# A fused encoder layer: one conv tap per fused pair on ScalarE, 64 fused pairs for 61, turned probabilities in the bias tile

## The chip, the cores and the metric

The kernel runs on one core of one Trainium2 chip, one launch for the whole layer. The metric is the time of the launch on the device in microseconds (us): 1574.34 us before, the median of 3 runs (1571.43 to 1574.68). All data are fp32; TensorE multiplies in its fp32r form, and each number is split into a high half and a low half, so that a product is three matmuls: high by high, low by high, high by low.

## The reference, cut to what matters

One encoder layer on 256 rows of 4096 columns. After a norm comes one projection of 4096 to 14336 columns, whose parts feed a convolution branch and an attention branch; both are gated, put side by side, and projected back to 4096.

```python
xn = rms_norm(x, norm_g[l])
h = jnp.einsum('bsd,de->bse', xn, w_in[l])                       # 256x4096 by 4096x14336
c_val, c_glu, c_gate, q, k, v, a_gate = jnp.split(h, split_pts, axis=-1)   # 7 x 2048
conv_out = conformer_conv(c_val, c_glu, ...) * jax.nn.silu(c_gate)   # GLU, depthwise conv of 31 taps, LayerNorm, SiLU
q = rms_norm(q.reshape(B, S, 16, 128), q_norm_g[l]); k = rms_norm(...)
attn = longnet_mixture(q, k, v, rel_bias)                        # 16 heads, three dilated windows, T5 bias
mixed = jnp.concatenate([conv_out, attn * jax.nn.silu(a_gate)], axis=-1)
x = x + jnp.einsum('bse,ed->bsd', mixed, w_out[l])               # 256x4096 by 4096x4096
```

In the kernel the three windows of the attention are one softmax over a 256x256 matrix of scores per head, with the pattern's weight folded into the bias.

## The kernel before

**Groups and pairs.** The weights of both projections are cut into 18 groups of 1024 columns, g0 to g17: four of the convolution's values and gates (g0 to g3), two of its outer gate (g4, g5), eight that alternate between queries with keys (`qk`) and attention gates with values (`agv`) in the order qk0, qk1, agv0, qk2, agv1, qk3, agv2, agv3 (g6 to g13), and four of the output projection (g14 to g17). A group has 16 pairs; a pair is 2x128 rows of weights by 1024 columns, loaded as one `raw` tile of 1 MB (`load_pair`, three tiles in flight). Its slot is its place in the group, its unit `u` is 16 times the group plus the slot, and the tiles carry the unit in their names (`wh219`). The group's four results, 128x512 each, stay in four PSUM banks while its 16 pairs go by; the other four banks (`side`) serve small matmuls of the side work.

**Plain and fused pairs.** A plain pair is 24 matmuls of 128x512: ScalarE casts the high half `wh` (L1027, two of 1024 columns), VectorE subtracts to get the low half `wl` (L1033, 2048 columns). A fused pair (`split_fused`, `fused`) multiplies its 2x2 blocks in the Strassen-Winograd way, with 7 products and so 21 matmuls; VectorE and ScalarE have to make sums of blocks for it, in four steps: `b` (one), `b22` (two), `t13` (three) and `t42` (four), each a cast on ScalarE and a subtraction on VectorE, with additions on VectorE between them (L1059, L1071, L1072), and four more PSUM banks hold its sums, so a group has no side banks while its fused pairs run. The sums of the rows' blocks come from `block_sums` once (`xs`, `xsp`). Before, groups 2 to 7 have six fused pairs, at slots 2, 4, 6, 8, 10 and 12, group 14 has four, and groups 15 to 17 have seven each, at slots 2, 4, 6, 8, 10, 12 and 13: 61 in all. Group 1 is plain and multiplies rows that aren't yet normalised; during it `split_xn` scales each of the 32 tiles of rows by its norm (L288, VectorE), casts (`nh`, L293, ScalarE) and subtracts (`nl`, L295).

**Side work and its order.** Everything else (the convolution, the attention, the gates, the splitting of the output projection's rows) is written as generators that wait in lanes. A planner emits them between the pairs: `credit` adds to `left[0]` (VectorE) and `left[1]` (ScalarE) for each matmul emitted (`PRODUCT`, 227 ns each, by the shares in `FILL`), `spend` takes off what an emitted operation is reckoned to cost, and `SAVED` is the most that can be kept. `pump` steps through the lanes; a lane steps while both its engines' credit is above zero. The order in which the operations are emitted is the order on each engine, and each engine takes its own queue in that order; weights are split ahead of their use as soon as `stream.step` finds storage: four tiles of 2048 columns, so a plain pair's halves are ready at most about one pair ahead, and four more of 1024 columns in the stretch of a group with fused pairs.

**The convolution's taps.** The 31 taps times four blocks of channels less the middle ones are 120 taps. Each is done either on VectorE (`conv_gen`, four operations L538) or on ScalarE (`conv_products`, four activations L500 into one of two `cp` buffers, then one addition L529 on VectorE). The lane `cp_lane` is stepped by `pump` and, in a fused pair, by step two of `split_fused`, after the cast of `b22`; a tap takes two steps.

**A head.** `head_gen` loads a Toeplitz tile of bias `T` (tag "toep", four buffers, 384 columns) over SP's queue, multiplies queries by keys into a side bank (`psc`, L701), adds bias (`pr`, L711), takes exponentials and scales on ScalarE (L718, L728), turns 32x32 blocks on VectorE (L734, into a tile `turn_p` of tag "t2", six buffers of 512 columns), writes that to DRAM and reads it back into `pr` over GpSimd's queue (`through_dram`), and multiplies by the values (`po`, L745).

## Time and profile before

| what | value |
|---|---|
| median of 3 runs | 1574.34 us (1571.43 to 1574.68) |
| the profiled execution | 1575.07 us |
| its span in the trace | 1573.3 us |
| TensorE busy (PE) | 1563.0 us, 99% |
| VectorE busy (DVE) | 1332.2 us, 85% |
| ScalarE busy (ACT) | 906.4 us, 58% |
| GpSimd busy (POOL) | 99.1 us, 6% |
| mean traffic of the DMA queues | 227 GB/s |

The span is from the first to the last record of the core; the profiled execution's time, measured as in the other runs, is 1.8 us longer. PE is TensorE, PEld its loads of stationary data, DVE VectorE, ACT ScalarE, POOL GpSimd, SP the engine whose queue issues most DMAs. A busy matmul record is longer than the step between two matmuls, since they are pipelined; how often a matmul starts is read from the starts or from windows. An arrow (`<-`) in brackets names what ended the idle time of the engine ahead of a row.

### The profile page before, as it was taken

To read this page: it belongs to the slowest core of one execution; us is meant where nothing else is said; L and a number is where in the kernel's file an instruction comes from. 1 tells how busy PE (TensorE), PEld (TensorE's weight loads), DVE (VectorE), ACT (ScalarE), POOL (GpSimd) and SP (SyncE) were. 2 spreads that over 40 slices of the span, in tenths; PEclk is the share of its full clock that TensorE was granted. 3 is DMA by queue.
4 is the path that set the end of the run, shared out by engine and by line. 5 is a ranking of instruction groups with operands and counts; after the bars stand their busy time and mean duration, and the time that the engine had idled before them with its cause. 6 is when DMAs were issued, how large, how long until landed. Compare 5 with 4: busy or idle time off the path is not lost.

```text
span 1573.3 us, 18566 instructions
## 1 busy us (share of the span) xinstructions
PE 1563.0 (99%) x6883; PEld 1293.3 (82%) x6883; DVE 1332.2 (85%) x1574; ACT 906.4 (58%) x1354; POOL 99.1 (6%) x184
## 2 busy tenths in 40 slices
PE   9999999999999999999999999999999999999999
PEld 8888788888888888888888887888888888888887
DVE  6667899989899998999878878888866788999988
ACT  6755554555455545667665775575565644555453
POOL 0000000000000000001202013021120300000000
PEclk9999999999999999999999999999999999999999
DMA  9766556555555565657967479566785765666663
GB/s 379 293 224 253 201 214 221 210 211 194 216 216 205 206 236 205 228 204 231 289 212 248 178 237 264 184 213 233 242 258 193 252 224 197 241 241 240 221 245 123
DMA packets 64523, 357.22 MB, mean 227 GB/s; under 512 B 9104, under 2 KB 11920, under 8 KB 27824
## 3 DMA queue, kind: packets, MB, share of 16 engines
q1 hardware_dynamic: 54096, 326.38, 58.3%
q0 software_dynamic: 10048, 29.37, 6.2%
q8 instruction: 54, 0.88, 0.2%
q10 hardware_dynamic: 288, 0.28, 0.1%
q14 instruction: 37, 0.30, 0.1%
HBM read 337.09 MB, written 18.91 MB: 226 GB/s over the span
## 4 chain that ended last, share of the span: by engine, by line
PE 98%; DMA 1%; issue 1%; DVE 1%; ACT 0%; POOL 0%; DVEq 0%; POOLq 0%
PE c L1226 44%; PE c L1228 22%; PE m L1197 5%; PE c L1242 4%; PE m L1199 3%; PE c L1244 2%; PE acc L929 2%; PE acc L930 2%; PE acc L932 2%; PE c L1088 2%; PE c L1089 2%; PE c L1197 2%; PE c L1090 2%; PE po L745 1%; PE m L1088 1%; PE c L1199 1%
## 5 line engine op out<-in xcount | busy, mean ns | idle before, releaser
L1033 DVE TENSOR_TENSOR wl<-raw,wh 128x2048 fp32r<-128x2048 f32 x211 | 482.8, 2289 | 155.5 <-ACT wh L1027 152.9
L1027 ACT CAST wh<-raw 128x1024 fp32r<-128x1024 f32 x422 | 421.3, 1048 | 241.7 <-PE c L1228 161.6
L1226 PE MATMUL c<-wh,nh 128*128 128x512 f32 x1152 | 449.1, 390 | 0.0
L1228 PE MATMUL c<-wh,nl 128*128 128x512 f32 x1152 | 448.2, 389 | 0.0
L1226 PE MATMUL c<-wl,nh 128*128 128x512 f32 x1152 | 285.9, 390 | 1.8 <-DVE wl L1033 1.8
L1050 ACT CAST t<-raw 128x1024 fp32r<-128x1024 f32 x122 | 128.5, 1053 | 267.0 <-DVE raw L1059 199.5
L1226 PEld LDWEIGHTS c<-wl,nh 128*128 128x128 f32 x1152 | 216.2, 188 | 47.1 <-DVE wl L1033 2.2
L1226 PEld LDWEIGHTS c<-wh,nh 128*128 128x128 f32 x1152 | 216.2, 188 | 44.9
L1228 PEld LDWEIGHTS c<-wh,nl 128*128 128x128 f32 x1152 | 216.2, 188 | 44.8
L1051 DVE TENSOR_TENSOR t<-raw,t 128x1024 fp32r<-128x1024 f32 x122 | 149.0, 1221 | 3.3
L538 DVE SCALAR_TENSOR_TENSOR cT<-a,wT,cT 128x255 f32<-128x255 f32 (+14 forms) x364 | 150.1, 471 | 0.3
L1226 PE MATMUL c<-wh,mh 128*128 128x512 f32 x280 | 109.1, 390 | 0.0
L1228 PE MATMUL c<-wh,ml 128*128 128x512 f32 x280 | 108.9, 389 | 0.0
L1059 DVE TENSOR_TENSOR raw<-raw 128x1024 f32<-128x1024 f32 x61 | 74.7, 1225 | 2.1
L1051 DVE TENSOR_TENSOR b<-raw,b 128x1024 fp32r<-128x1024 f32 x61 | 74.3, 1218 | 0.1
L1226 PE MATMUL c<-wl,mh 128*128 128x512 f32 x280 | 69.1, 389 | 0.0
L1050 ACT CAST b<-raw 128x1024 fp32r<-128x1024 f32 x61 | 63.9, 1047 | 1.3 <-DMA raw<-in_w_dram 0.9
L1226 PEld LDWEIGHTS c<-wl,mh 128*128 128x128 f32 x280 | 52.6, 188 | 10.9
L1226 PEld LDWEIGHTS c<-wh,mh 128*128 128x128 f32 x280 | 52.6, 188 | 10.9
L1228 PEld LDWEIGHTS c<-wh,ml 128*128 128x128 f32 x280 | 52.6, 188 | 10.9
L1197 PE MATMUL m<-t,xsp 128*128 128x512 f32 x180 | 60.3, 389 | 0.0
L1003 DVE TENSOR_TENSOR wh<-raw,wh 128x1024 fp32r<-128x1024 f32 x31 | 37.9, 1224 | 26.1 <-ACT wh L1002 25.9
(329 smaller groups left out, 2210.2 us busy)
## 6 DMA issues: line engine op xcount, KB each, us to landing
raw<-in_w_dram SPq DMA_DIRECT2D x286, 1024.0 KB, 4.9
xT<-in_x_cols_dram SPq DMA_DIRECT2D x15, 512.0 KB, 6.9
x<-in_x_dram SPq DMA_DIRECT2D x8, 512.0 KB, 7.8
xr<-in_x_dram SPq DMA_DIRECT2D x8, 512.0 KB, 6.5
out_dram<-xr SPq DMA_DIRECT2D x15, 256.0 KB, 7.0
T<-bias_dram SPq DMA_DIRECT2D x16, 192.0 KB, 6.4
raw<-in_w_dram SPq DMA_DIRECT2D x3, 512.0 KB, 6.0
turn_qk0d<-turn_qk POOLq DMA_DIRECT2D x2, 512.0 KB, 5.9
```

What stands on the lines that cost most here:

```text
L538: nc.vector.scalar_tensor_tensor(c[:, t, lo:hi], a[:, t, lo + sh : hi + sh], wT[:, 4 * cb + t, k : k + 1], c[:, t, lo:hi], op0=ALU.mult, o ...
L1027: nc.scalar.copy(h, raw_tiles[u][:, k])
L1033: nc.vector.tensor_sub(l, src, h.bitcast(F32))
L1050: nc.scalar.copy(h, src)
L1051: nc.vector.tensor_sub(l, src, h.bitcast(F32))
L1059: nc.vector.tensor_add(r[:, 0:4:3, :], r[:, 0:3:2, :], twice(r[:, 3, :]))
L1088: nc.tensor.matmul(acc, a[0], b[0], start=start, stop=False)
L1197: nc.tensor.matmul(acc, ah, b, start=begin, stop=end)
L1199: nc.tensor.matmul(acc, al, b, start=False, stop=False)
L1226: nc.tensor.matmul(acc, a[s][0], b[e], start=begin, stop=False)
L1228: nc.tensor.matmul(acc, a[s][1], b[e], start=False, stop=False)
L1242: nc.tensor.matmul(acc, a[s][0], b[e], start=False, stop=end)
```

## The change

- `N_FUSED`, `FUSED`: groups 2 to 7 have 5, 7, 7, 7, 7 and 6 fused pairs, where each had 6; the seventh is at slot 13. That is 64 in all. The sums of pairs 12 and 13 lie in small tiles of tag "toep", which are widened from 384 to 512 columns; tag "t2" has five buffers for six.
- In step two of a fused pair (`two`), `left[1]` is lifted to at least 1, so that `cp_lane` takes its two steps whenever it has a tap and a buffer is free: one tap on ScalarE per fused pair. Before, each step asked for over 800 ns of credit. `pump` takes up to two steps above `CP_MIN` = 300 instead of one above 1500. `FILL` and `SAVED` give more credit, to ScalarE above all.
- In program order 63 of the 120 taps stand on ScalarE after the change, 29 before; 21 loads of activation tables after, 15 before.
- `tmp = T`: the turned probabilities go into the head's own bias tile.
- `split_xn` takes two empty steps between the multiplication and the cast.
- `state["held"]` counts side banks in use; a group starts only when they are released, and side work may ask for banks until two slots earlier in a group without fused pairs. `channel_mean` waits as `settled` does; `qk_norm` waits for ScalarE's credit; `post_lane` looks at VectorE's credit alone; the head lane comes behind the post lane.

ScalarE at the end of group 1: casts of normalised rows (`nh`), of plain pairs (`wh`, by unit; `wh31` is the last of the group) and of sums (`xsp`). Before:

```order
L293 CAST nh21_1396<-xT20_1215 128x256
L293 CAST nh22_1427<-xT20_1215 128x256
L293 CAST nh23_1430<-xT20_1215 128x256
L1027 CAST wh30_1433<-raw30_1311 128x1024 x2
L334 CAST xsp10_1460<-xs_10_1424 128x512
L293 CAST nh24_1472<-xT24_1307 128x256
L1027 CAST wh31_1476<-raw31_1358 128x1024 x2
L293 CAST nh25_1488<-xT24_1307 128x256
L1132 ACTIVATE warm_68<-ones_66 128x1
L293 CAST nh26_1518<-xT24_1307 128x256
L293 CAST nh27_1521<-xT24_1307 128x256
```

After:

```order
L301 CAST nh19_1406<-xT16_1115 128x256
L301 CAST nh20_1409<-xT20_1202 128x256
L1051 CAST wh30_1412<-raw30_1294 128x1024 x2
L342 CAST xsp8_1423<-xs_8_1389 128x512
L1051 CAST wh31_1451<-raw31_1339 128x1024 x2
L1159 ACTIVATE warm_68<-ones_66 128x1
L301 CAST nh21_1476<-xT20_1202 128x256
L301 CAST nh22_1488<-xT20_1202 128x256
L301 CAST nh23_1491<-xT20_1202 128x256
L1051 CAST wh32_1494<-raw32_1379 128x1024 x2
L301 CAST nh24_1510<-xT24_1290 128x256
```

In front of `wh31` there stood `nh24` and the casts before it; now the last cast of a row ahead of `wh31` is `nh20`, and `nh21` to `nh24` stand behind it.

VectorE at the end of group 10 (units 160 to 175), where the probabilities of heads 5 to 7 (`pr5` to `pr7`) are turned; `wl` are the low halves, `cT2` rows are taps of the convolution, `turn_qk` and `turn_ag` other transpositions. Before:

```order
L1033 TENSOR_TENSOR wl173_7236<-raw173_7096,wh173_7219 128x2048
L429 STREAM_TRANSPOSE turn_qk21_7215<-qk2_1_6643 128x4x4x32
L734 STREAM_TRANSPOSE turn_p5_7257<-pr5_6822 128x4x4x32
L734 STREAM_TRANSPOSE turn_p6_7278<-pr6_6827 128x4x4x32
L734 STREAM_TRANSPOSE turn_p7_7280<-pr7_6898 128x4x4x32
L538 SCALAR_TENSOR_TENSOR cT2_6371<-a2_6273,wT_73,cT2_6371 128x246
L1033 TENSOR_TENSOR wl174_7283<-raw174_7141,wh174_7261 128x2048
L538 SCALAR_TENSOR_TENSOR cT2_6371<-a2_6273,wT_73,cT2_6371 128x246
L529 TENSOR_TENSOR cT2_6371<-cT2_6371,cp0_77 128x4x244
L529 TENSOR_TENSOR cT2_6371<-cT2_6371,cp1_78 128x4x245
L1033 TENSOR_TENSOR wl175_7324<-raw175_7192,wh175_7311 128x2048
```

After:

```order
L1057 TENSOR_TENSOR wl175_7352<-raw175_7215,wh175_7338 128x2048
L751 STREAM_TRANSPOSE T5_6542<-pr5_6962 128x4x4x32
L751 STREAM_TRANSPOSE T6_6544<-pr6_7014 128x4x4x32
L537 TENSOR_TENSOR cT2_6624<-cT2_6624,cp1_78 128x4x246
L546 SCALAR_TENSOR_TENSOR cT2_6624<-a2_6540,wT_73,cT2_6624 128x248
...
L546 SCALAR_TENSOR_TENSOR cT2_6624<-a2_6540,wT_73,cT2_6624 128x248 x4
L1057 TENSOR_TENSOR wl178_7495<-raw178_7354,wh178_7481 128x2048
L751 STREAM_TRANSPOSE T7_6558<-pr7_7060 128x4x4x32
L537 TENSOR_TENSOR cT2_6624<-cT2_6624,cp1_78 128x4x247
```

The three transpositions stood in a row ahead of `wl174` and `wl175` and wrote into tiles of their own; now two stand behind `wl175`, the third behind `wl178` in group 11, and they write into `T5`, `T6` and `T7`.

ScalarE in slots 12 and 13 of group 5 (units 92 and 93). Before:

```order
L1050 CAST b_920_3751<-raw92_3671 128x1024
L1066 CAST b22_92_3756<-raw92_3671 128x512
L1050 CAST t13_92_3774<-raw92_3671 128x1024
L1050 CAST t42_92_3779<-raw92_3671 128x1024
L1027 CAST wh93_3800<-raw93_3710 128x1024 x2
L1027 CAST wh94_3834<-raw94_3743 128x1024 x2
```

After:

```order
L1074 CAST b_920_3757<-raw92_3676 128x1024
L1090 CAST b22_92_3762<-raw92_3676 128x512
L1074 CAST t13_92_3780<-raw92_3676 128x1024
L1074 CAST t42_92_3785<-raw92_3676 128x1024
L1074 CAST b_93_3806<-raw93_3715 128x1024
L1090 CAST b22_93_3810<-raw93_3715 128x512
L508 ACTIVATE cp0_77<-a0_1054,wT_73 128x244 x4
L1074 CAST t13_93_3827<-raw93_3715 128x1024
L1074 CAST t42_930_3836<-raw93_3715 128x1024
L1051 CAST wh94_3855<-raw94_3749 128x1024 x2
```

Unit 93 was plain and is fused, and the four activations of one tap stand between its `b22` and its `t13`.

The diff:

```diff
 PRODUCT = 227
-FILL, SAVED = ((0.97, 0.76), (1.0, 0.93)), (700, 700)
+FILL, SAVED = ((0.97, 0.85), (1.0, 0.97)), (700, 1500)
 RAW = 3
...
 SETTLED = 3000
+CP_MIN = 300
 C4 = 16
...
 FUSED_IN = range(2, 8)
-FUSED = [(2, 4, 6, 8, 10, 12) if g in FUSED_IN else () for g in range(N_IN)]
+N_FUSED = dict(zip(FUSED_IN, (5, 7, 7, 7, 7, 6)))
+FUSED = [(2, 4, 6, 8, 10, 12, 13)[: N_FUSED.get(g, 0)] for g in range(N_IN)]
+SUMS = max(FUSED)
 FUSED += [range(4)] + 3 * [range(7)]
...
-    state = {"side": "side", "taps": True}
+    state = {"side": "side", "taps": True, "held": 0}
     const = ctx.enter_context(tc.tile_pool(name="const", bufs=1))
...
     def t2(name):
-        return sb.tile([P, 512], F32, tag="t2", bufs=6, name=name)
+        return sb.tile([P, 512], F32, tag="t2", bufs=5, name=name)
...
     def side(name):
+        state["held"] += 1
         return ps.tile([P, 512], F32, tag=state["side"], bufs=4, name=name)
...
         yield 480
+        yield 0
+        yield 0
         h, l = new_split(k, "n")
...
         yield 415
-        if k % 2 and k // 2 in FUSED[FUSED_IN[0]]:
+        if k % 2 and k // 2 in SUMS:
             yield from block_sums(
                 k // 2, src_of=xT, parts=(xnh, xnl), out=xsum, name="xs",
-                small=k // 2 == FUSED[FUSED_IN[0]][-1],
+                small=k // 2 in SUMS[5:],
             )
...
         if small:
-            both = [sb.tile([P, 512], F32R, tag="t2", bufs=6, name=f"{name}p{j}{i}") for i in "hl"]
+            both = [sb.tile([P, 512], F32R, tag="toep", bufs=4, name=f"{name}p{j}{i}") for i in "hl"]
         else:
...
         tot = flat[:, :S]
-        yield
-        yield
+        yield from settled()
         while not state["side"]:
...
         nc.scalar.copy(mu, pm[:, :S])
+        state["held"] -= 1
         yield 0, 400
...
         pv = yield from channel_mean(sq, "va", sq[0])
-        r = yield from rsqrt(pv[:, :S], [P, S], 1.0, LN_EPS, "rc")
+        steps = rsqrt(pv[:, :S], [P, S], 1.0, LN_EPS, "rc")
+        cost = next(steps)
+        state["held"] -= 1
+        yield cost
+        r = yield from steps
         for cb in range(4):
...
             for n in range(8):
+                while left[1] <= 0:
+                    yield
                 junk = sb.tile([P, DH], F32, tag="junk", bufs=1, name=f"sq{hg}_{i}_{n}")
...
             for n in range(8):
+                while left[1] <= 0:
+                    yield
                 w_ = v[:, DH * n : DH * n + DH]
...
             yield
-        T = sb.tile([P, 384], F32, tag="toep", bufs=4, name=f"T{h}")
+        T = sb.tile([P, 512], F32, tag="toep", bufs=4, name=f"T{h}")
         nc.sync.dma_start(
-            T,
+            T[:, :384],
             bass.AP(
...
         nc.vector.scalar_tensor_tensor(pi, psc, SCALE, window, op0=ALU.mult, op1=ALU.add)
+        state["held"] -= 1
         nm = sb.tile([P, 2], F32, tag="st", bufs=8, name=f"nm{h}")
...
         yield from settled()
-        tmp = t2(f"turn_p{h}")
+        tmp = T
         nc.vector.transpose(
...
         nc.vector.tensor_mul(m, m, by_block(po[:, :S]))
+        state["held"] -= 1
         mix_ready[h] = m
...
-    post_lane, head_lane, gate_lane, mix_lane = Lane(2), Lane(4), Lane(1, ()), Lane(1)
+    post_lane, head_lane, gate_lane, mix_lane = Lane(2, (0,)), Lane(4), Lane(1, ()), Lane(1)
     fetch_lane, ag_lane = Lane(1, (1,)), Lane(1, ())
...
+    lanes = (
+        gate_lane, fetch_lane, ag_lane, post_lane, head_lane, ln_lane, ln_lane, post_lane,
+        mix_lane, mix_lane,
+    )
     def pump(more=0):
...
             split_more()
-        for lane in (gate_lane, fetch_lane, ag_lane, ln_lane, ln_lane, post_lane, head_lane, post_lane, mix_lane, mix_lane):
+        for lane in lanes:
             lane.step(left, spend)
...
                 break
-        if left[1] > 1500 and state["taps"] and not split_gens:
-            cp_lane.step(left, spend)
+        for _ in range(2):
+            if left[1] > CP_MIN and state["taps"] and not split_gens:
+                cp_lane.step(left, spend)
         for i in range(2):
...
                 for _ in range(2):
-                    if left[1] > 800:
-                        cp_lane.step(left, spend)
+                    left[1] = max(left[1], 1)
+                    cp_lane.step(left, spend)
                 nc.vector.tensor_sub(l, r[:, 2, :], h.bitcast(F32))
...
                 rows = xh, xl
+            while state["held"]:
+                state["side"] = None
+                pump(PRODUCT)
             one = {n: self.bank(g, n, tags[0]) for n in ("c11", "c21", "c12", "c22")}
...
             firsts = [s for s, j in enumerate(ORDERS[g]) if j in FUSED[g]]
-            window = range(1, (firsts + [n_pairs - 1])[0])
+            window = range(1, (firsts + [n_pairs - 3])[0])
             for slot, j in enumerate(ORDERS[g]):
...
         nc.tensor.matmul(spin[:, :P], ones, ones, start=True, stop=True)
+    state["held"] = 0
```

## Rows read from the trace of the kernel before

**Rows 1.** The first part of the page (busy time, share of the span, instructions) of all engines, and the chain that ended last, by engine.

```profile
PE 1563.0 (99%) x6883; PEld 1293.3 (82%) x6883; DVE 1332.2 (85%) x1574; ACT 906.4 (58%) x1354; POOL 99.1 (6%) x184
...
PE 98%; DMA 1%; issue 1%; DVE 1%; ACT 0%; POOL 0%; DVEq 0%; POOLq 0%
```

**Rows 2.** Windows of the program: the stretch, its length, then of PE, PEld, DVE, ACT and POOL the busy time with the number of instructions, the granted clock of TensorE, the share of the DMA engines and GB/s. The stretches are group 1 with the end of group 0, group 2, group 10, and group 16.

```profile
93.00:183.10 90.10, 88.51 (x389) 71.73 (x388) 67.65 (x105) 45.93 (x70) 2.88 (x5) 1.00 0.67 241
183.10:266.20 83.10, 83.10 (x368) 68.83 (x367) 78.45 (x87) 43.06 (x51) 0.56 (x1) 1.00 0.57 209
...
862.10:958.70 96.60, 92.77 (x402) 76.13 (x401) 75.15 (x104) 65.27 (x134) 14.76 (x27) 0.98 0.64 206
...
1404.90:1487.20 82.30, 82.30 (x364) 68.15 (x364) 76.52 (x74) 43.10 (x48) 0.00 (x0) 1.00 0.65 232
```

**Rows 3.** The waits of TensorE by line and by what it waited for: us in total, times, the longest.

```profile
PE c L1242 <- DVE wl L1033: 3.6, 2, 2.0
PE c L1226 <- DVE wl L1033: 1.8, 1, 1.8
```

**Rows 4.** The timeline at the end of group 1 (start, us, engine, line, operation, tiles, number, and the idle time ahead with its releaser), ScalarE's and VectorE's rows ahead of a wait of TensorE, and that wait.

```profile
173.68 0.41 ACT L293 CAST nh<-xT 128x256 fp32r<-128x256 f32 x1 [2.28 <-issue]
...
173.99 1.99 ACT L1027 CAST wh<-raw 128x1024 fp32r<-128x1024 f32 x2
...
176.02 2.29 DVE L1033 TENSOR_TENSOR wl<-raw,wh 128x2048 fp32r<-128x2048 f32 x1 [1.08 <-ACT wh L1027]
...
178.36 0.50 PE L1242 MATMUL c<-wl,xh 128*128 128x512 f32 x1 [1.59 <-DVE wl L1033]
```

**Rows 5.** The timeline at the end of group 10, columns as in rows 4.

```profile
933.98 1.26 DVE L734 STREAM_TRANSPOSE turn_p<-pr 128x512 f32<-128x512 f32 x2
...
943.86 0.71 DVE L734 STREAM_TRANSPOSE turn_p<-pr 128x512 f32<-128x512 f32 x1 [8.62 <-DMA turn_p5d<-turn_p]
...
944.85 2.29 DVE L1033 TENSOR_TENSOR wl<-raw,wh 128x2048 fp32r<-128x2048 f32 x1
...
947.19 2.14 PE L1226 MATMUL c<-wl,nh 128*128 128x512 f32 x8 [1.80 <-DVE wl L1033]
...
952.27 1.02 PE L1242 MATMUL c<-wl,nh 128*128 128x512 f32 x2 [2.02 <-DVE wl L1033]
```

**Rows 6.** VectorE's groups of instructions by line: shapes, number, busy us and mean ns of one, idle us ahead and what ended most of it.

```profile
L538 DVE SCALAR_TENSOR_TENSOR cT<-a,wT,cT 128x255 f32<-128x255 f32 (+14 forms) x364 | 150.1, 471 | 0.3
L1051 DVE TENSOR_TENSOR t<-raw,t 128x1024 fp32r<-128x1024 f32 x122 | 149.0, 1221 | 3.3
L1059 DVE TENSOR_TENSOR raw<-raw 128x1024 f32<-128x1024 f32 x61 | 74.7, 1225 | 2.1
...
L1070 DVE TENSOR_TENSOR b<-raw,b 128x512 fp32r<-128x512 f32 x61 | 41.7, 684 | 0.0
...
L529 DVE TENSOR_TENSOR cT<-cT,cp 128x964 f32<-128x964 f32 (+4 forms) x29 | 33.8, 1165 | 1.2
...
L734 DVE STREAM_TRANSPOSE turn_p<-pr 128x512 f32<-128x512 f32 x16 | 10.9, 694 | 19.1 <-DMA turn_p5d<-turn_p 8.6 <-DMA turn_p0d<-turn_p 5.6 <-DMA turn_p8d<-turn_p 4.9
```

**Rows 7.** The timeline around slot 13 of group 15.

```profile
1388.38 1.05 ACT L1050 CAST t<-raw 128x1024 fp32r<-128x1024 f32 x1 [2.27 <-DVE raw L1059]
...
1390.26 2.43 DVE L1051 TENSOR_TENSOR t<-raw,t 128x1024 fp32r<-128x1024 f32 x2
...
1392.95 0.84 PE L1197 MATMUL m<-t,msp 128*128 128x512 f32 x3
```

**Rows 8.** ScalarE's groups of instructions by line, columns as in rows 6.

```profile
L1050 ACT CAST t<-raw 128x1024 fp32r<-128x1024 f32 x122 | 128.5, 1053 | 267.0 <-DVE raw L1059 199.5 <-DVE raw L1072 58.8 <-PE c L1228 7.7
...
L500 ACT ACTIVATE cp<-a,wT 128x241 f32<-128x241 f32 (+4 forms) x116 | 49.2, 488 | 10.1 <-DVE cT L529 10.1
...
L611 ACT ACTIVATE cT<-cT,vec_cols 128x256 f32<-128x256 f32 x16 | 8.6, 592 | 0.0
...
L718 ACT ACT_TABLE_LOAD x4 | 5.1, 1283 | 0.1
```

**Rows 9.** TensorE's group of the scores, columns as in rows 6.

```profile
L701 PE MATMUL psc<-qk,near_q 128*128 128x256 f32 x64 | 14.5, 379 | 0.0
```

**Rows 10.** Windows at the end of group 10, TensorE's columns first as in rows 2.

```profile
952.00:956.00 4.00, 3.73 (x9) 2.95 (x10) 3.86 (x4) 1.02 (x3) 0.69 (x2) 0.57 1.05 227
956.00:960.00 4.00, 4.00 (x19) 3.29 (x18) 0.35 (x1) 2.35 (x4) 1.38 (x3) 1.00 1.02 264
```

**Rows 11.** The timeline at the multiplications by the last heads' values, the loads of weights (PEld) alone.

```profile
1260.69 0.73 PEld L745 LDWEIGHTS po<-pr,agv 128*128 128x128 f32 x4 [0.33 <-issue]
```

**Rows 12.** The timeline in group 13, around a load of an activation table, a cast of a plain pair and the use of that cast.

```profile
1196.77 1.28 ACT L718 ACT_TABLE_LOAD   x1
...
1198.07 0.51 ACT L718 ACTIVATE pr<-pr,nm 128x256 f32<-128x256 f32 x1
...
1200.19 2.00 ACT L1027 CAST wh<-raw 128x1024 fp32r<-128x1024 f32 x2 [1.03 <-PE c L1228]
...
1207.24 0.39 PE L1226 MATMUL c<-wh,nh 128*128 128x512 f32 x1
```

## The prediction, made before the changed kernel had run

> **What bounds the kernel now.** I read the page first: the share of each engine and the chain that ended last [rows 1]. TensorE is busy for 1563.0 of 1573.3 us and makes up 98% of the chain; VectorE is at 85%, ScalarE at 58%. So the time is the number of matmuls, plus the places where TensorE stands. Next come the windows by group of weights [rows 2], to price a matmul and to find those places: group 2, which holds six fused pairs and ten plain ones (6×21 + 10×24 = 366 matmuls), takes 83.1 us with TensorE busy throughout, 0.227 us each. Group 16, with seven fused pairs (363 matmuls), takes 82.3 us, 0.2267 each, and here too nothing is lost. The two other windows lose time: group 1 (with a tail of group 0) and group 10. The waits of TensorE [rows 3] name the cause of both: three waits for `wl`, the low halves of a plain pair's weights, 1.8 + 3.6 us.
>
> The timeline of the end of group 1 [rows 4] shows how the first arises. ScalarE reaches the cast `nh` of a normalised row, which stands ahead of the cast `wh` in its queue, and stands for 2.28 us; `wh` therefore starts at 173.99 and is done at 175.98, VectorE can form `wl` only from 176.02 to 178.31, and TensorE takes it up at 178.36, having stood 1.59 us. In the timeline of the end of group 10 [rows 5], VectorE stands 8.62 us ahead of one transposition `turn_p`: its output needs a t2 buffer, and that buffer is still read by the write to DRAM of `turn_p5`. Behind it in VectorE's queue stands `wl` (944.85), and TensorE waits 1.80 us for that and 2.02 us for the next.
>
> **The matmuls removed.** Three more fused pairs, each with 21 matmuls in place of 24: 9×0.227 = **−2.0 us**. This is on the path wherever TensorE is the bound, so it counts in full, if the other two engines can make the parts. Forming a fused pair costs VectorE three subtractions and one addition of 1024 columns and three operations of 512: 4×1.22 + 3×0.68 = 6.9 us against 2.29 for a plain `wl` [rows 4, 6], so three more cost 3×4.6 = 14 us. The seven-pair pattern, with pairs at slots 12 and 13 in a row, is new in groups 3 to 6, but it already runs in groups 15 to 17, in the window of group 16 at no loss [rows 2]. How thin that is, the timeline of such a place in group 15 shows [rows 7]: ScalarE stands 2.27 us ahead of the cast of `t13`, VectorE ends the low halves at 1392.69, and TensorE begins its multiplications by them at 1392.95, a row of three, of which the third, 2×0.227 later, is the first that needs the half ended last: 0.7 us to spare.
>
> **The taps.** In the program order, 63 taps of 120 stand on ScalarE after, 29 before: 34 more. A tap on VectorE is four operations of 0.471 us = 1.88 us; on ScalarE it is four of 0.488 = 1.95 us there and an addition of 1.165 us on VectorE [rows 6, 8]. So VectorE is relieved of 34×(1.88−1.17) = 24 us and ScalarE loaded with 34×1.95 = 66 us. With the fused pairs VectorE comes to 1332 + 14 − 24 = 1322 us (84%), ScalarE to 906 + 66 and some 13 for the casts of three fused pairs and six table loads = 985 us (63%). Neither is the bound by its sum, so by sums this is worth nothing either way; TensorE had all it needed in the fused groups already. The question is where the forced tap stands: between the casts of `b22` and `t13`. ScalarE now stands there 199.5 us for VectorE's L1059 over 61 pairs, 3.3 us each [rows 8], and 2.27 us in the tight place [rows 7]; a tap of 1.95 us goes into this hole. I count it at zero, with the price if the hole is too short among the rivals. The Trainium skill speaks against the tap ("ScalarE: Activation LUTs", section "Rules for kernel authors"): it says that multiplications belong on VectorE and not on ScalarE. In fp32 the rows here show 0.488 against 0.471 us per 250 columns, no such distance; by the rule the sum would be the same, since ScalarE's time is not on the path.
>
> **The normalised rows (group 1).** Two empty steps hold the cast of a row back behind its multiplication, and with it later rows fall behind the `wh` that TensorE needs. In the order of after, `wh31` stands ahead of `nh21`, where before it stood behind `nh24`; the row's input is long there. So the wait of 2.28 us falls out and `wh` starts some 2 us earlier, which covers the 1.59. The window is 90.10 us for 389 matmuls, of which 389×0.227 = 88.2 are needed: **−1.9 us**. Lower bound of the gain: 0, if another queue entry takes the place of `nh`; upper: the 1.9.
>
> **The turned probabilities (group 10).** They now go into T, the tile of the bias, whose last reader, the addition L711 of the same head, is long past when the transposition comes; no t2 tile is asked for, so the wait of 8.62 us has no reason left. All waits of this kind come to 19.1 us of VectorE [rows 6]; only those of group 10 reach TensorE. What goes: group 10 is 384 matmuls and 16 of scores, at 14.5/64 = 0.227 us each [rows 9], 400×0.227 = 90.8 us, and its window takes 96.6: **−5.8 us**. Of these 3.8 are the two waits. Most of the rest is the slow stretch behind them [rows 10]: from 952 to 956, granted clock 0.57, 9 matmuls start in 4 us where 956 to 960 at full clock starts 19. TensorE had stood 2 us twice ahead of it and then ran at its level of 1.2 GHz; without the standing there is no cause for that. What is late next: `wl` of the pair after is cast from weights that had landed, and the storage, four tiles, lets VectorE run up to a pair ahead, so nothing is. T tiles are asked for at issue on SP's queue, ahead of weight loads; their predecessors' writes are heads long past in the order, so the weights behind them don't wait. T's pool now also holds the four tiles of the sums of pairs 12 and 13, until their last fused pairs in groups 7 and 6; by the order the loads that take these tiles come well behind those. One t2 tile fewer (5) stands against one tile per head that no longer asks for one.
>
> **Moves that I count at zero.** The side banks held until released, the empty slots at a group's end, and the head lane behind the post lane move additions and small matmuls by one or two pumps; the side work's readers have 5 us or more between its production and its use. Bounds: +0 to +2 us, from the shortest distance that I saw, the `po` of L745, where weights already waited 0.33 us [rows 11].
>
> **Sum.** 1575.07 (profiled run) − 2.0 − 1.9 − 5.8 = 1565.4. The profiled run is 0.7 us above the median of 1574.34, so for the median **1564.5 us** (rounded down a little, as small gaps of the same kind go with the large ones).
>
> **Rivals.** *Rival 1, ScalarE late at the table switches.* The order after has 21 table loads instead of 15, and in group 13 three of them, with two SiLU, four exponentials and two casts, between the casts of two plain pairs: 3×1.28 + 2×0.59 + 4×0.51 + 2.0 = 9.1 us of ScalarE [rows 8, 12], against 5.44 of TensorE per pair (24×0.227). Before, the cast of a pair ended 5.05 us ahead of its use (1200.19 + 2.00 to 1207.24) [rows 12], so the lead falls to some 1.5 us and the `wl` behind it would just be on time. If a load costs more than its row, TensorE waits 2 to 4 us here and at the end of group 8, where four loads stand between two casts: 1567 to 1570. For it: the lead is small, and half-clock stretches follow a stand. Against it: the row after the load starts at once, 1196.77 + 1.28 to 1198.07. The Trainium skill ("ScalarE: Activation LUTs", section "What ACT_TABLE_LOAD costs") gives a drain of about 1.38 us on top of the load, 2.66 us for a switch, by which the three loads would take an estimated 4 us more and bring this rival in full. By that page, the trace does not agree: between the load and the next activation there is 0.02 us. Chance 0.13.
> *Rival 2, the probabilities' round trip is late.* If turning after the weights (T5, T6 behind `wl175`, T7 behind `wl178`) delays a write and its read-back, the matmul `po` waits at TensorE's head: 1 to 4 us, 1566 to 1569. Against: 5 us and more of distance by the order. Chance 0.08.
> *Rival 3, it does not do what it says.* VectorE's stand in group 10 moves to another buffer or transfer and stays 5.8: 1575.1 − 2.0 − 1.9 − 0.7 = 1570.5. Chance 0.06.
> *Rival 4, slower: the tap stands in the path.* In slots 12 and 13 of four seven-pair groups, `t13` is delayed by the tap if its buffer is not free: taps have waited for the addition that frees it, 10.1 us in all [rows 8]. With the waits of ScalarE gone and 2×1.95 us in the path, less 1.0 us to spare (0.3 of the hole, 0.7 at TensorE), TensorE stands 2.9 us per group, and the half clock of [rows 10] costs 1.7 more (4 us, 9 starts, 0.27 of it a wait): 4×4.6 = 18 us, 1583. It decides as soon as the tap with its wait is longer than the hole by over 0.7 us. Chance 0.08.
>
> **How the numbers follow.** Forecast 0.62 (1563.5 to 1566), rival 1 0.13, rival 2 0.08, rival 3 0.06, rival 4 0.08, others 0.03. A run of this kernel can't be told from no change within 0.2%, 3.1 us: faster is below 1571.2. Rival 3 lies at that bound and is halved. Faster: 0.62 + 0.13 + 0.08 + 0.03 = 0.86; same: 0.03 of rival 3 and 0.02 of others, 0.05; slower: rival 4 and the last 0.01, 0.09. Eight in ten lies between 1562.0 (all waits gone, and runs as low as 1571.43 against the median) and 1571.0, which leaves out rival 4 and others.
>
> **What would show it.** Windows of groups 3 to 6 at 82.3 us or so; group 1 at 88 and group 10 at 91 us with no granted clock below 1; no wait of TensorE for `wl`; no idle ahead of L751's transposition; and ScalarE near 985, VectorE near 1322 us. It is wrong if TensorE's waits name `t` or `b` of fused pairs (rival 4), `wh` or `wl` in groups 8 and 13 (rival 1), `po` (rival 2), or if VectorE still stands for a DMA ahead of a `wl` (rival 3).

## The result, and the profile after

The changed kernel takes 1565.66 us, median of 4 runs (1565.24 to 1565.90), against 1574.51 us (1571.43 to 1575.94) for the kernel before. The ratio is 0.9946 with a 95% interval of 0.9929 to 0.9963: faster by 8.9 us, clear of the interval. The forecast was 1564.5 us, in a range of 1562.0 to 1571.0. The profiled execution took 1565.90 us with a span of 1564.1 us; before, 1575.07 and 1573.3. The spans differ by 9.2 us, and the terms below add up to that.

The page after: its first part, and the chain that ended last by engine, which answer to [rows 1].

```profile
PE 1559.1 (100%) x6874; PEld 1290.6 (83%) x6874; DVE 1335.1 (85%) x1495; ACT 971.0 (62%) x1503; POOL 98.9 (6%) x184
...
PE 99%; DMA 0%; DVE 0%; SPq 0%; ACT 0%; DVEq 0%; issue 0%
```

The waits of TensorE after, all of them; the row in place of those of [rows 3] is gone, and what is left is the start of the program:

```profile
PE spin L1326 <- DVE ones L169: 1.1, 1, 1.1
```

Windows by group after, columns as in [rows 2]: group 1 with the end of group 0, group 2, group 4, group 8, group 10 and group 16.

```profile
93.00:181.20 88.20, 88.20 (x391) 73.04 (x390) 65.15 (x95) 45.23 (x67) 2.87 (x5) 1.00 0.72 252
181.20:264.80 83.60, 83.60 (x371) 69.22 (x370) 75.99 (x88) 44.73 (x56) 0.56 (x1) 1.00 0.58 208
347.30:429.80 82.50, 82.50 (x365) 68.18 (x364) 76.83 (x72) 49.40 (x60) 0.53 (x1) 1.00 0.58 210
677.80:768.30 90.50, 90.50 (x402) 75.13 (x401) 79.07 (x103) 70.14 (x147) 13.18 (x24) 1.00 0.78 248
859.80:949.40 89.60, 89.60 (x397) 74.28 (x396) 80.51 (x102) 73.82 (x156) 11.55 (x21) 1.00 0.69 228
...
1395.70:1478.00 82.30, 82.30 (x365) 68.17 (x364) 76.45 (x74) 43.07 (x48) 0.00 (x0) 1.00 0.64 231
```

TensorE is busy for the whole of each window, and the granted clock is 1.00 in all. A group is taken here to end where its last matmul's record ends: group 1 at 181.2 us instead of 183.2. The six groups with fused pairs take 181.2 to 677.8, 496.6 us, where they took 183.2 to 681.0, 497.8. Groups 8 to 13 take 677.8 to 1225.6, 547.8 us, where they took 681.0 to 1234.6, 553.6. They must be taken together, since 16 matmuls of scores have moved to group 8, 12 of them from group 9 and 4 from group 10. From there to the end it is 0.2 less. So 2.0 + 1.2 + 5.8 + 0.2 = 9.2 us.

The timeline after at the end of group 1 (against [rows 4]) and then at the turned probabilities in group 10 (against [rows 5]):

```profile
168.59 2.00 ACT L1051 CAST wh<-raw 128x1024 fp32r<-128x1024 f32 x2 [2.92 <-issue]
...
170.59 1.01 ACT L301 CAST nh<-xT 128x256 fp32r<-128x256 f32 x3
170.62 2.29 DVE L1057 TENSOR_TENSOR wl<-raw,wh 128x2048 fp32r<-128x2048 f32 x1 [0.97 <-ACT wh L1051]
...
941.03 1.30 DVE L751 STREAM_TRANSPOSE T<-pr 128x512 f32<-128x512 f32 x2
942.25 1.14 DVE L537 TENSOR_TENSOR cT<-cT,cp 128x984 f32<-128x984 f32 x1
...
944.59 2.29 DVE L1057 TENSOR_TENSOR wl<-raw,wh 128x2048 fp32r<-128x2048 f32 x1 [0.68 <-ACT wh L1051]
```

The casts of rows come behind the last `wh` of group 1 and don't wait; that `wh` is done at 170.59, where it was done at 175.98, and its `wl` at 172.91. VectorE turns two probabilities with no idle time ahead, and goes on.

### The profile page after: what moved, and what is told of

It is laid out like the page before. It is cut to its first block, busy times and chain, and to the rows that moved or that the text cites. A ratio compares the mean times of both kernels' runs of the same rounds, so it can differ in the third digit from the quotient of the medians.

```text
span 1564.1 us, 18620 instructions
## 1 busy us (share of the span) xinstructions
PE 1559.1 (100%) x6874; PEld 1290.6 (83%) x6874; DVE 1335.1 (85%) x1495; ACT 971.0 (62%) x1503; POOL 98.9 (6%) x184
## 4 chain that ended last, share of the span: by engine, by line
PE 99%; DMA 0%; DVE 0%; SPq 0%; ACT 0%; DVEq 0%; issue 0%
PE c L1253 44%; PE c L1255 22%; PE m L1224 6%; PE c L1269 4%; PE m L1226 3%; PE c L1271 2%; PE c L1114 2%; PE c L1112 2%; PE c L1224 2%; PE c L1113 2%; PE acc L956 2%; PE acc L953 2%; PE acc L954 2%; PE m L1114 1%; PE c L1226 1%; PE m L1113 1%
## 5 line engine op out<-in xcount | busy, mean ns | idle before, releaser
L1057 DVE TENSOR_TENSOR wl<-raw,wh 128x2048 fp32r<-128x2048 f32 x208 | 475.7, 2289 | 150.2 <-ACT wh L1051 140.9
L1051 ACT CAST wh<-raw 128x1024 fp32r<-128x1024 f32 x416 | 414.9, 1048 | 222.1 <-PE c L1255 134.7
L1253 PE MATMUL c<-wh,nh 128*128 128x512 f32 x1128 | 439.6, 390 | 0.0
L1255 PE MATMUL c<-wh,nl 128*128 128x512 f32 x1128 | 438.9, 389 | 0.0
L1074 ACT CAST t<-raw 128x1024 fp32r<-128x1024 f32 x128 | 134.9, 1054 | 253.9 <-DVE raw L1083 190.5
L1253 PE MATMUL c<-wl,nh 128*128 128x512 f32 x1128 | 280.5, 391 | 0.0
L1075 DVE TENSOR_TENSOR t<-raw,t 128x1024 fp32r<-128x1024 f32 x128 | 156.2, 1221 | 3.6 <-ACT t L1074 0.3
L508 ACT ACTIVATE cp<-a,wT 128x241 f32<-128x241 f32 (+8 forms) x252 | 105.6, 490 | 6.4 <-DVE cT L537 6.3
L546 DVE SCALAR_TENSOR_TENSOR cT<-a,wT,cT 128x255 f32<-128x255 f32 (+7 forms) x228 | 95.1, 473 | 0.5
L1083 DVE TENSOR_TENSOR raw<-raw 128x1024 f32<-128x1024 f32 x64 | 78.4, 1225 | 2.2
L537 DVE TENSOR_TENSOR cT<-cT,cp 128x964 f32<-128x964 f32 (+8 forms) x63 | 73.8, 1172 | 2.8 <-DVE cT L537 0.5
```

The lines of the kernel that those rows point to most:

```text
L508: nc.scalar.activation(cp[:, t, lo:hi], a[:, t, lo + sh : hi + sh], AF.Copy, scale=wT[:, 4 * cb + t, k : k + 1],)
L537: nc.vector.tensor_add(c[:, :, lo:hi], c[:, :, lo:hi], cp[:, :, lo:hi])
L546: nc.vector.scalar_tensor_tensor(c[:, t, lo:hi], a[:, t, lo + sh : hi + sh], wT[:, 4 * cb + t, k : k + 1], c[:, t, lo:hi], op0=ALU.mult, o ...
L1051: nc.scalar.copy(h, raw_tiles[u][:, k])
L1057: nc.vector.tensor_sub(l, src, h.bitcast(F32))
L1074: nc.scalar.copy(h, src)
```

## The experiments

Each ran in one go with runs of the kernel before on the same chip; medians of five runs, except where a number is given. The medians of the kernel before lie between 1574.18 and 1575.10 us in these goes, so times of different goes compare to about 1 us.

**The tile alone.** The kernel before with this edit; the order on every engine stays as it was.

```diff
-        return sb.tile([P, 512], F32, tag="t2", bufs=6, name=name)
+        return sb.tile([P, 512], F32, tag="t2", bufs=5, name=name)
...
-        T = sb.tile([P, 384], F32, tag="toep", bufs=4, name=f"T{h}")
+        T = sb.tile([P, 512], F32, tag="toep", bufs=4, name=f"T{h}")
...
-        tmp = t2(f"turn_p{h}")
+        tmp = T
```

> The kernel before with one part of the change alone: the turned probabilities go into the bias tile T (512 columns for 384), and t2 has five buffers for six to make room. Every instruction stands where it stood before on all engines. Theory (the stand of VectorE in group 10 came from the t2 buffer, and costs TensorE its waits and the half clock behind them): 1574.5 - 5.8 = 1568.7 us, group 10 at 90.8 us, no idle time ahead of the transpositions. Rival (the gain of the change in group 10 came from the new places of the transpositions, not from the tile): 1574.5 us, with the stand at another buffer.

Measured: 1569.64 us (before 1574.98), ratio 0.9968, interval 0.9955 to 0.9980. The window of group 10, and VectorE's timeline there:

```profile
862.10:952.60 90.50, 90.50 (x401) 75.13 (x400) 75.21 (x104) 65.28 (x134) 14.25 (x26) 1.00 0.68 222
```
```profile
933.91 1.86 DVE L734 STREAM_TRANSPOSE T<-pr 128x512 f32<-128x512 f32 x3
```

All three transpositions in a row, without the stand; group 10 is 6.1 us shorter, with the clock at 1.00, and the wait for `wl` in group 1 (1.6 us) is still there. With the order unchanged, the t2 buffer was the cause of the stand, and the two waits and the half clock behind it went with it.

**All but the tile.** Two kernels with the same order on every engine: the changed kernel with 61 fused pairs (`N_FUSED` six times 6), and that one without the tile (t2 with six buffers, T of 384 columns, the sums of pair 12 in t2).

> The changed kernel with six fused pairs in each of groups 2 to 7, as before: 61 in all, 9 matmuls more. Theory (a matmul left out is worth its 0.227 us): 1565.7 + 2.0 = 1567.7 us. Rival (pairs at slots 12 and 13 in a row cost what they save): 1565.7 us.

> The run of 61 fused pairs without the tile: the turned probabilities go to t2 (six buffers), the order on every engine is that run's. First theory (under the new order the t2 buffers are free in time wherever TensorE would feel it): 1569.5 us within 1 us. Second theory (the tile is needed under the new order too): over 1572 us, with waits of TensorE for wl behind a transposition.

Measured: with the tile 1569.53 us (8 runs, 1569.16 to 1571.00), ratio to before 0.9971 (0.9961 to 0.9982); without it 1568.94 us, ratio 0.9961 (0.9949 to 0.9973). VectorE's waits for transposition buffers without the tile:

```profile
DVE turn_p L751 <- DMA turn_p8d<-turn_p: 5.0, 1, 5.0
...
DVE turn_p L751 <- DMA turn_p12d<-turn_p: 2.1, 1, 2.1
```

VectorE still stands, the longest time ahead of the third of three transpositions in a row (heads 8 to 10, from 1044.0 us; the kernel before stands there too, for 4.9 us, and TensorE doesn't feel it), but TensorE's waits are the same two as with the tile. So under this order the tile is worth nothing: it and the order are two cures for one illness, and the second theory falls. This order is that of 61 pairs, in which heads 4 to 7 are turned one at a time (from 852.4, 863.5, 923.1 and 928.8 us with the tile); the changed kernel turns heads 5 and 6 together, and its own order was not run without the tile. The other expectation failed too, by 1.9 us: 61 pairs cost 3.9 us more than 64, not 2.0. The windows of group 2 with six pairs, in this kernel and then in the run with one empty step (below), and TensorE's waits in this kernel, show why:

```profile
180.80:266.30 85.50, 84.27 (x368) 68.55 (x367) 76.98 (x83) 45.62 (x57) 0.56 (x1) 1.00 0.56 203
```
```profile
180.90:263.90 83.00, 83.00 (x368) 68.75 (x367) 76.38 (x85) 43.06 (x51) 0.56 (x1) 1.00 0.56 203
```
```profile
PE c L1255 <- DVE nl L303: 0.7, 1, 0.7
PE c L1113 <- DVE xsp12l L344: 0.4, 1, 0.4
```

The last normalised rows and their sums come during group 2. With five fused pairs the changed kernel has no wait there, with six it has. The second empty step is only a part of this: with one step and six pairs in the changed kernel, group 2 still takes 84.2 us ("More fused pairs", below).

**Without the empty steps.** The changed kernel less these two lines:

```diff
         yield 480
-        yield 0
-        yield 0
         h, l = new_split(k, "n")
```

> The changed kernel without the two empty steps of split_xn; nh21 to nh24 then stand ahead of wh31 again on ScalarE. Theory: ScalarE stands ahead of nh again and wh31 is late, TensorE waits 1.6 us for wl, with small parts 1.9: 1565.7 + 1.9 = 1567.6 us. Rival (group 1 gained by the other moves, such as the planner's credits): 1565.7 us and no wait of TensorE.

Measured: 1573.09 us (11 runs, 1571.54 to 1576.18), ratio 0.9992 (0.9983 to 1.0001): 7.4 us slower than after, not 1.9. TensorE's waits in the profiled run, of 1571.54 us:

```profile
PE po L760 <- DMA pr<-turn_p15d: 1.8, 1, 1.8
PE c L1267 <- DVE wl L1055: 1.6, 1, 1.6
...
PE po L760 <- DMA pr<-turn_p14d: 0.5, 1, 0.5
```

The wait of group 1 is back with its 1.6 us; group 1 ends at 184.2, 3.0 later than after. Without the two steps the planner also put the write of `turn_ag3` ahead of all reads of the last four heads' probabilities on GpSimd's queue, and that queue stood for it:

```profile
1234.85 0.54 POOL L402 DMA_DIRECT2D turn_ag3d<-turn_ag  x1 [7.80 <-DVE turn_ag L435]
1235.46 0.56 POOL L409 DMA_DIRECT2D pr<-turn_p12d  x1
```

Besides, `po` of head 15 stands earlier in TensorE's order, right behind that of the other three heads (1255.41 us); the changed kernel has 96 matmuls between them (1249.53 and 1271.56). `po` waits, group 14 takes 90.6 us where it took 87.8, and 2.8 us are lost there; how much of that is the queue and how much the place of `po`, no run separates. The two places are 5.8 us, about the 5.6 by which the profiled runs differ. The profiled run is the fastest of the 11; where the others lose up to 4.6 us more, no trace shows.

**The tile and one empty step.** The kernel before with the tile, and one empty step in place of two.

> The kernel before with the tile T for the turned probabilities, as in the run of the tile alone, and one empty step in split_xn instead of two, so that nh24 stands behind wh31 on ScalarE. Everything else as before, but for a few side operations that move by a pump. Theory (the wait of group 1 comes from nh24 ahead of wh31): the run of the tile alone less 1.9 us, 1569.6 - 1.9 = 1567.7 us, group 1 ends at 181.3 us and no wait of TensorE is left. Rival (another cast takes the place of nh24): 1569.6 us with a wait for wl at the end of group 1.

Measured: 1566.97 us (1566.66 to 1567.98), ratio 0.9956 (0.9943 to 0.9968). TensorE's only wait is that of the start, and group 1 ends at 180.9. One edit and one line of code are thus 7.2 us of the 8.9; credits, the forced tap, the held banks and the lanes are not in this kernel. It has 61 fused pairs, and is 2.6 us faster than the changed kernel with 61 pairs (1569.53): its group 2 takes 83.0 us and not 85.5. The rest of the change buys no time in these runs beyond the three more pairs.

**The tap not forced.**

```diff
-                    left[1] = max(left[1], 1)
-                    cp_lane.step(left, spend)
+                    if left[1] > 800:
+                        cp_lane.step(left, spend)
```

> The changed kernel with the tap of a fused pair asked for only when ScalarE has over 800 ns of credit, as before. 64 taps then stand on ScalarE, one more than after, at other places. Theory (the taps are beside the path either way): 1565.7 us within 1 us, no wait of TensorE. Rival (the forced tap keeps VectorE free in the later groups, so that TensorE waits without it): over 1568 us, with waits for wl or wh in groups 8 to 13.

Measured: 1566.02 us (1565.27 to 1567.27), ratio 0.9944 (0.9932 to 0.9957): no difference in time. But TensorE has a wait, where the theory had none:

```profile
PE po L762 <- DMA pr<-turn_p0d: 0.7, 1, 0.7
```

The wait for `po` is not one of those that the rival named. In the program order of the changed kernel only 12 of the 64 fused pairs hold a tap at all, 7 of them at slot 2 or 13, and not one each: a tap needs one of the two `cp` buffers, and the addition that frees one is emitted by `pump`, between plain pairs. The other 51 taps of ScalarE stand between pairs.

**How large the hole is.** The changed kernel with n idle activations in each of the 64 fused pairs, n = 7 and n = 14:

```diff
                     left[1] = max(left[1], 1)
                     cp_lane.step(left, spend)
+                for i in range(n):
+                    nc.scalar.activation(
+                        sb.tile([P, DH], F32, tag="junk", bufs=1, name=f"idle{u}_{i}"), ones, AF.Copy
+                    )
```

> The changed kernel with seven more activations of 128x128 into a scratch tile in every fused pair, between the casts of b22 and t13: by the nearest row (0.31 us for 128x128) about 2.1 us of ScalarE each, as much as one tap, in all 64 pairs and not only in those that hold a tap. They compute nothing. Theory (ScalarE stands some 3 us ahead of t13 for VectorE, and that hole takes a tap): 1565.7 us within 1 us. Rival (the tap stands in the path in slots 12 and 13, where the hole is smaller): about 1.1 us and a restart for each of seven groups, 1575 us or more, with waits of TensorE for t or b.

> As the run with seven, with fourteen such activations, about 4.3 us of ScalarE in every fused pair. Theory (the hole of 3 us and the 0.7 us ahead of TensorE are what hides a tap): late by 0.6 us in an ordinary fused pair and 1.3 us in slot 13, so 1575 us at the least (seven groups) and 1605 us at the most (all 64 pairs), waits of TensorE for t. Rival (the parts of a fused pair are made so early that ScalarE's place there doesn't matter): 1566 us.

Measured: with seven, 1565.43 us (1565.30 to 1565.91), ratio 0.9945 (0.9932 to 0.9959): as the changed kernel. With fourteen, 1591.11 us (4 runs), ratio 1.0107 (1.0093 to 1.0121): 25.5 us slower. ScalarE's groups with seven, columns as in [rows 8]:

```profile
L1095 ACT ACTIVATE idle<-ones 128x128 f32<-128x128 f32 x448 | 139.0, 310 | 12.1
L1074 ACT CAST t<-raw 128x1024 fp32r<-128x1024 f32 x128 | 134.2, 1052 | 112.7 <-DVE raw L1083 56.3 <-DVE raw L1100 55.4 <-PE c L1259 1.0
```

In the changed kernel ScalarE stood 190.5 us ahead of `t13` for L1083; now 56.3. The 139 us of idle work went into the hole, all but 5 us of it. With fourteen, the waits of TensorE and the timeline of slot 13 of group 3:

```profile
PE m L1228 <- ACT t L1074: 15.6, 9, 3.9
```
```profile
334.75 1.98 ACT L1074 CAST t<-raw 128x1024 fp32r<-128x1024 f32 x2
335.81 2.36 DVE L1075 TENSOR_TENSOR t<-raw,t 128x1024 fp32r<-128x1024 f32 x2 [2.94 <-ACT t L1074]
...
335.83 0.50 PE L1228 MATMUL m<-t,xsp13h 128*128 128x512 f32 x1 [2.61 <-ACT t L1074]
```

Now VectorE waits for ScalarE, and TensorE for both: 9 waits, not 64. Five are at slot 13, where one fused pair follows another, in groups 3, 4, 5, 6 and 15, with 1.1 to 3.9 us each; slot 13 of groups 16 and 17 has none. The other four are in group 7, which has no pair at slot 13, ahead of its pairs at slots 4, 6, 8 and 10:

```profile
PE m L1228 <- ACT t L1074: 2.8, 4, 0.9
```

So the hole is too short at most of the places where one fused pair follows another, and at four in group 7; elsewhere the lead covers it. Why group 7 has less of a lead was not tried. The 15.6 us of waits are less than the 25.5 lost; group 5, from 435.3 to 525.0, has a granted clock of 0.96 over its 89.7 us.

**The credits alone.** The kernel before with the new `FILL` and `SAVED`.

> The kernel before with the planner's credits alone (FILL and SAVED): 46 taps on ScalarE instead of 29, and VectorE turns the probabilities of heads 4 and 5 behind wl158 and of heads 6 and 7 behind wl165 and wl166, instead of 5, 6 and 7 in a row behind wl173; they still go to t2 buffers. First theory (the stand needs three transpositions in a row without a free t2 buffer, and another order is as good a cure as the tile): group 10 at 90.8 us, 1574.3 - 5.8 = 1568.5 us, with the 1.6 us wait of group 1 still there. Second theory (only the tile cures it): 1574.3 us, with a stand of VectorE ahead of a transposition in group 9 or 10 that TensorE feels.

Measured: 1582.35 us, ratio 1.0043 (1.0030 to 1.0056): slower by 7.3 us. Both theories fail. Groups 9 and 10, and three of TensorE's waits:

```profile
772.90:876.40 103.50, 98.00 (x417) 80.15 (x417) 81.00 (x103) 63.18 (x112) 21.45 (x39) 0.95 0.70 216
876.40:963.50 87.10, 87.10 (x386) 72.13 (x385) 78.47 (x111) 64.95 (x130) 13.20 (x24) 1.00 0.74 234
```
```profile
PE po L745 <- DMA pr<-turn_p1d: 3.1, 1, 3.1
...
PE po L745 <- DMA pr<-turn_p0d: 2.4, 1, 2.4
PE mupm L574 <- DVE mutot L566: 1.9, 1, 1.9
```

The stand in group 10 is indeed gone with the tile as it was. But with side work emitted earlier, `po` stands in TensorE's queue in group 9, and a mean over channels in group 12, before their operands are there, and group 9 has a granted clock of 0.95. The changed kernel has the same credits without these waits, so something else in it keeps them off. Whether that is the held banks, `channel_mean` that waits, the order of the lanes or another part was not tried.

**More fused pairs.** First `N_FUSED` = (6, 7, 7, 7, 7, 7) in the changed kernel; then the same with one empty step; then 7 in group 2 as well, with one empty step.

> The changed kernel with 6, 7, 7, 7, 7, 7 fused pairs in groups 2 to 7: 66 in all, 6 matmuls fewer. Theory (TensorE is the bound everywhere and the other two engines follow): 1565.7 - 6 x 0.227 = 1564.3 us. Rival (in group 2 the normalised rows and their sums aren't ready for a sixth pair, or the side work that group 7 no longer holds crowds group 8): a wait of TensorE of 1.4 us or more, 1565.7 us or above.

> The changed kernel with one empty step in split_xn instead of two, so that rows are ready a pump earlier, and 6, 7, 7, 7, 7, 7 fused pairs, 66 in all. Theory (the sixth pair of group 2 failed for the second empty step, as the run of the tile with one step had 83.0 us in group 2 with six pairs): 1565.7 - 6 x 0.227 = 1564.3 us, no wait of TensorE in group 2. Rival (group 2 can't feed six fused pairs in this order either): 1567.5 us with waits for nl or xsp.

> As the run of 66 pairs, with a seventh pair in group 2, at slot 13: 67 in all. Theory: 1565.7 - 9 x 0.227 = 1563.6 us. Rival (the rows and sums of pair 13 come last, from the end of group 1, and TensorE meets them): a wait of 1 us or more in group 2, 1565 us or above.

Measured: 1567.69 us, ratio 0.9954 (0.9941 to 0.9966); 1565.90 us (1565.68 to 1566.82), ratio 0.9942 (0.9931 to 0.9954); and 1571.83 us (12 runs, 1567.01 to 1575.14), ratio 0.9975 (0.9964 to 0.9986). The rival held in the first and the third; the second lies halfway between the theory's 1564.3 us and the rival's 1567.5, with the wait for `nl` that the rival named. TensorE's waits in group 2 of the first, of the second and of the third:

```profile
PE c L1255 <- DVE nl L303: 1.2, 1, 1.2
...
PE c L1269 <- ACT nh L301: 0.6, 1, 0.6
PE c L1113 <- DVE xsp12l L344: 0.3, 1, 0.3
```
```profile
PE c L1254 <- DVE nl L302: 0.8, 1, 0.8
```
```profile
PE c L1111 <- ACT xsp13h L341: 1.8, 1, 1.8
```

Six fewer matmuls are worth 1.4 us. Group 2 with six pairs takes 86.4 us in the first and 84.2 in the second, where 83.0 is possible (above), and so gives that back to rows that aren't ready. The first two differ by one empty step, which is thus worth 2.2 us in group 2; the other 1.2 above 83.0 come from other parts of the change, and no run says which. The third spreads over 8 us; its profiled run, of 1567.32, has that wait and a group 2 of 86.2 us, and no trace shows why others take up to 1575.14. None of these beats the changed kernel.

## Why the prediction was right

**The turned probabilities, −5.8 us.** Groups 8 to 13 gave 5.8. The mechanism (t2 buffer, stand, late `wl`, half clock) is shown by the tile alone, 6.1 us in its profile and 5.3 in the medians. What the prediction did not see is that a new order can be a second cure: in the order of 61 pairs, with the transpositions behind other weights, leaving out the tile costs TensorE nothing. For the order of the changed kernel itself this is likely, but not shown, so how the 5.8 us divide between tile and order there stays open.

**The normalised rows, −1.9 us.** 2.0 in the profile, with some luck: group 1 itself, from its first matmul to that of group 2, shrank from 89.5 to 87.0 us, 2.5, since smaller stands ahead of the large one went too, and group 0 ended 0.5 us later. (389×0.227 is 88.3 and not 88.2, so by its own price the term was −1.8.) The run with one empty step shows the mechanism in the kernel before (group 1 ends 2.3 us earlier, 180.9 for 183.2, its wait gone), and the run without the steps brings the wait back. What was missing was the price in group 2: rows that come later. The prediction took five pairs there as one fewer and did not ask why.

**The matmuls removed, −2.0 us.** This was the mis-sized term: it brought 1.2. The count of matmuls is right, and group 2 is 0.6 us longer for its one pair less (83.6 against 83.0), as counted. But groups 3 to 6 take 82.5 us where 363 matmuls at 0.2267 are 82.3, the time of group 16; this is four times 0.2 us, told at the end. The prediction took the seven-pair pattern of groups 15 to 17 as proof that it costs nothing, but there the sums lie in other tiles.

**The taps, 0.** Right, and more firmly than argued: with an extra 2.1 us of ScalarE in every fused pair the time doesn't change. The reckoning of the hole (3.3 us, 2.27 in the tight place, 0.7 behind it) stands: 2.1 us fit and 4.3 do not, and 12.9 of the 15.6 us of waits arise at slot 13. But the place was less in use than the prediction took it to be, with 12 taps in 64 pairs. The sums of busy time were off: VectorE came to 1335 us, not 1322, ScalarE to 971, not 985. One tap operation starts before the record of the one ahead has ended, on VectorE 78 to 91 ns before, so the busy time of a group is less than its number times the mean of one. The group of 364 in [rows 6] is 150.1 us of busy time, 0.412 each where the mean is 0.471. That a tap relieves VectorE by 0.7 us was thus too much; 0.412×4 − 1.165 is 0.48, which for 34 taps is 8 of the 13 us.

**The moves counted at zero.** Together they are near zero: groups 14 to 17 lost nothing, and groups 8 to 13 gained what the stand had cost. They are not idle, though: the credits, which the prediction doesn't price, made the kernel 7.3 us slower without the rest of the change, with `po` late by 3.1 and 2.4 us. The bound of 2 us, which the prediction took from [rows 11], had no ground there; the 0.33 us in that row is idle time of the loads, not a distance between a result and its use.

**Rival 1** was reckoned closely and did not come. The timeline after in group 13, between the casts of two plain pairs (ScalarE), and the first use of the second (TensorE):

```profile
1191.15 2.00 ACT L1051 CAST wh<-raw 128x1024 fp32r<-128x1024 f32 x2
1193.17 1.28 ACT L623 ACT_TABLE_LOAD   x1
1194.46 0.60 ACT L623 ACTIVATE cT<-cT,vec_cols 128x256 f32<-128x256 f32 x1
1195.08 1.28 ACT L735 ACT_TABLE_LOAD   x1
...
1198.46 1.28 ACT L623 ACT_TABLE_LOAD   x1
1199.76 0.60 ACT L623 ACTIVATE cT<-cT,vec_cols 128x256 f32<-128x256 f32 x1
1200.27 1.98 ACT L1051 CAST wh<-raw 128x1024 fp32r<-128x1024 f32 x2
...
1203.60 0.39 PE L1253 MATMUL c<-wh,nh 128*128 128x512 f32 x1
```

From 1193.15 to 1202.25 are 9.1 us, as predicted, and the cast is done 1.35 us ahead of its use. Each load is followed by its activation 0.01 to 0.02 us later. The Trainium skill ("ScalarE: Activation LUTs", section "What ACT_TABLE_LOAD costs") counts a drain of about 1.38 us to each switch. The trace doesn't agree: no such time appears behind these loads, nor ahead of them, and three of them, an estimate of 4.1 us, would have made the cast late. The measurement decides.

**Rival 2** did not come in the changed kernel, but late reads for `po` did in the run without the empty steps, which lost 2.8 us there, in that of the credits alone, with waits of 3.1 and 2.4 us, and with 0.7 us where the tap was not forced. So the distance depends on where the planner puts the writes, the reads and `po`, and which of these decides was not separated. **Rivals 3 and 4** fell with the tile alone and with the seven idle activations.

## What to carry to other kernels

Where an engine stands ahead of an instruction for a buffer, look for a tile whose last reader is past: here the exchange alone, with no instruction moved, brought 5.3 us, and under another order nothing. In a kernel whose order comes from a planner, a part of a change can be no more judged by taking it out than by putting it in: taking out two empty steps moved a DMA and a matmul in another group and cost 2.8 us there, so read windows by stage, not only the total. And sum busy time from a group's total, not from its number times the mean duration, when its instructions follow each other closely.

## What the runs showed of the hardware

The 0.2 us in groups 3 to 6 sits in the matmuls of pairs 12 and 13, whose sums of rows lie in the tiles of tag "toep". Matmuls that read these sums as stationary data take longer from one start to the next. The changed kernel; then the two kernels of "All but the tile", with the same order on every engine, first with the sums of pair 12 in "toep" and then in t2 (duration in ns: least, median, most):

```profile
L1224 PE MATMUL m<-t,xsp12h x30: 392/394/404, 328.6 to 660.9; 128*128 128x512 f32 x30
L1112 PE MATMUL c<-b,xsp12h x5: 404/404/404, 327.9 to 657.8; 128*128 128x512 f32 x5
```
```profile
L1224 PE MATMUL m<-t,xsp12h x36: 392/394/405, 245.4 to 664.7; 128*128 128x512 f32 x36
L1224 PE MATMUL m<-t,xsp12h x36: 389/389/397, 245.2 to 664.0; 128*128 128x512 f32 x36
```

In group 4 after, 26 matmuls of these two pairs start 230 to 241 ns after the one ahead instead of 227, 184 ns more in all, the same ones in both pairs. With 61 pairs there are 13 such starts and 93 ns in that group with the sums in "toep", and none in t2. So it goes with the tiles in which these sums lie. The loads of weights take 188 ns in all three kernels. What it is about these tiles that costs this (their place, their size, a neighbour in use) was not tried.
